# Gate blocks of a hybrid layer in a second lane beside the differential heads

## The chip, the cores and the metric

The kernel runs on one core of a Trainium2 chip. The metric is the device time of one execution in microseconds. TensorE's matmuls stand as PE in the profile and its weight loads as PEld; VectorE is DVE, ScalarE is ACT, GpSimd is POOL, and SP issues the DMAs.

## The reference

A sequence of 1024 tokens with 1024 features goes through two hybrid layers and then through two layers of a second block (S5 and stick-breaking attention, an MLP, gates and a pooling mixer). The change is in the hybrid layers alone. Each of them does this:

```python
h = rms_norm(x, norm_g) * (1.0 + scale) + shift
proj = h @ w_in                                  # 1024 x 3360
c_q, c_kv, k_pe, na_qkv, diff_qkv, g_mla, g_na, g_diff = split(proj)
...                                              # 6 MLA heads, 6 neighborhood heads, 4 differential heads
a = softmax(q0 @ k0) - lam * softmax(q1 @ k1)    # each differential head has two score maps
...
y = concat([o_mla * silu(g_mla), o_na * silu(g_na), o_d * silu(g_diff)]) @ w_out
return x + gate * y
```

The three gates are the last 1024 columns of `proj`: eight blocks of 128 features. Blocks 0 to 2 belong to the MLA heads, 3 to 5 to the neighborhood heads, 6 and 7 to the differential heads.

## The kernel before

All products are computed in fp32 by splitting each operand into a rounded part and a rest (`fp32r`), and three matmuls stand for one (`mm3`). A weight block is loaded (`wr`), its rounded part is a cast on ACT (`wh`, line 293) and its rest a subtraction on POOL (`wl`, line 294). The normalized input `hT` is held in 16 of the 43 pages of 4 KB per partition that the pool `pg` has; PSUM holds two score buffers of two banks (`big`, tile S) and four single banks (`mm`, also used for transposes and products).

A layer is a list of stages, and a stage is a list of items, generators whose parts are separated by `yield`. `lane` starts one item per turn and moves the items begun earlier on by one part, so that work of several items interleaves. While a stage's items run, the preparation steps of the next stage (loads and splits of its weights) are emitted, spread over those items. `run` can emit a second lane beside the first (`side`): its steps are spread evenly over the items of a given number of stages of the first lane. Up to now only a later part of the network uses it. From this emission the framework makes the order in which each engine is served, using times that it estimates (`schedule_with_timeline_sim=True`); the order is then fixed, each engine works through its own list, and the framework puts in the waits.

The stages of a hybrid layer in order: latent projections (`lat`); two gate stages of four blocks each, in which an MLA projection item (`mla_item`) alternates with two gate items (`gate_item`, lines 682 to 695); values and queries and keys of the other heads (`dv`, `dqk`, `nq`, `nk`, `nv`); the four differential heads, the six neighborhood heads, the six MLA heads; the output projection. A gate item takes 24 matmuls of 128x512 for one block and one half of the tokens, copies the product on ACT (line 691), computes the sigmoid (lines 340 to 345: two DVE operations and three activations), multiplies (line 693) and stores the gate to DRAM, from where the heads load it per pair of heads. Gate weights come as two halves of 512 columns, each in four loads of 512 KB.

A differential head has 16 items, one for each block of 128 queries and each of its two score maps: two matmuls of 512 columns into a score buffer (line 1070), the minimum on DVE, which also frees the buffer (line 790), the exponential on ACT (line 793), scaling on POOL (line 798) or DVE (line 1080), the addition of the two maps on POOL (line 1077), then, `lag` turns later, eight transposes (line 813) with copies on ACT (line 819), and, `lag2` turns after those of the second query block, the product with the values (line 839).

Of the kernel before, what the change touches and what calls it, by code (L numbers as in the profile page):

```python
# [9 lines left out]
F32 = mybir.dt.float32  # L10
F32R = mybir.dt.float32r
# [7 lines left out]
NT = 8  # L19
EPS = 1e-6  # L20

LEAD = {0: 4, 1: 8}
TABLES = "natural_log_exp_and_others"

CM = 3
# [79 lines left out]
class Weights:  # L105
# [12 lines left out]
    def load(self, j):  # L118
        N = self.N
        raw = self.new(F32, (128, self.kper, self.cols), name="wr")  # L120
        self.raw[j] = raw
        self.parts(raw, j * self.kper, self.kper)
# [38 lines left out]
class Net:  # L161
# [518 lines left out]
            self.dma(dst[t], v)  # L680
        return f

    def gate_item(self, W, b, n, hT, dst):
        def f():
            bs = slice(b * 128, b * 128 + 128)
            p = self.mm()
            self.mm3(p, [(W.hi(k)[:, bs], W.lo(k)[:, bs], hT.half("h", k, n), hT.half("l", k, n)) for k in range(8)])
            yield
            x = self.half(name="gx")
            g = self.half(name="gate")  # L690
            self.nc.scalar.copy(x, p)
            yield from self.sigmoid(g, x)
            self.nc.vector.tensor_mul(g, x, g)
            self.dma(dst[:, n * 512:n * 512 + 512], g)
        return f

    def project1(self, i, hT, early=None):
        I = self.I
        w_in = I["w_in"][i]
        D = {k: self.scratch(s, F32, name=f"{k}{i}") for k, s in {  # L700
            "mq": [6, 2, 96, S], "mk": [6, 2, 96, S], "mv": [NT, 128, 768],
            "nq": [2, 3, 128, S], "nk": [2, 3, 128, S], "nv": [NT, 128, 768],
            "dqk": [2, 4, 128, S], "dv": [NT, 128, 256], "g": [8, 128, S]}.items()}
        L = {}
# [19 lines left out]
        prep = []  # L724
# [9 lines left out]
        W = W0 = self.weights(w_in[:, 0:416], 416)  # L734
# [5 lines left out]
        else:  # L740
            ws.insert(0, gains)
        stages = [Stage(ws, [self.lat_item(t, hT, W, L) for t in range(NT)], "lat")]
        for c in (1, 0):
            W = self.weights(w_in[:, 2336 + c * 512:2848 + c * 512], 512)
            items = []
            for b in range(4):
                items += [self.mla_item((1 - c) * 4 + b, L, D)]
                items += [self.gate_item(W, b, n, hT, D["g"][c * 4 + b]) for n in range(2)]
            stages.append(Stage((prep if c else []) + W.steps(1), items, f"gate{c}", LEAD[c]))
        W = self.weights(w_in[:, 2080:2336], 256)  # L750
        stages.append(Stage(W.steps(), [self.v_plain(t, hT, W, 4, D["dv"]) for t in range(NT)], "dv"))

# [13 lines left out]
        stages.append(Stage(W.steps(), qk(W, 384, heads((0, 6, 64, "nk", False)), D["nk"]), "nk"))  # L766
        W = self.weights(w_in[:, 1184:1568], 384)
        stages.append(Stage(W.steps(), [self.v_item(t, hT, W, 6, D["nv"]) for t in range(NT)], "nv"))
        return D, stages


    def head_rows(self, src, h, d, ws, name):
# [264 lines left out]
    def diff_stages(self, i, D, mixT):  # L1037
# [45 lines left out]
        def sub(M):  # L1083
# [8 lines left out]
            yield  # L1092
            nc.vector.tensor_mul(M, M, sq)
            nc.vector.tensor_scalar_mul(M, M, C["sg"])
        st = self.attn_stages(4, 6, loads, tile, self.full_pair, D["dv"], D, mixT, sub=sub, subs=2, plain=True, lag=9, lag2=3)
        st[0].prep.insert(0, consts)
        return st

# [58 lines left out]
    def block1(self):  # L1157
# [17 lines left out]
            C["A"], C["B"] = self.rows(I["ln_mix_even_2"][0], "mA"), None  # L1175
        P, loads, products, ends = self.ada_rows()
        early = []
        D, st = self.project1(0, hT, early)

        begun = {}  # L1180

# [9 lines left out]
        stages = [Stage(pre, [lambda t=t: begun.pop(t) if t in begun else norm0(t) for t in range(NT)], "norm")]  # L1191
        for i in range(2):
            if i == 1:
                D, st = self.project1(i, hT)
            nf, E = self.na_bias(i)
            st[3].prep += nf
            stages += st
            if i == 0:
                ad = self.ada_steps(0, mods[0], (2,)) + self.ada_steps(1, mods[1])
                for j in range(4, 8):  # L1200
                    st[j].prep += ad[(j - 4) * len(ad) // 4:(j - 3) * len(ad) // 4]
            mixT = FeatT(self, "mx")
            df = self.diff_stages(i, D, mixT)
            na = self.na_stages(D, mixT, E)
            ml = self.mla_stages(D, mixT)
            if i == 1:
                T = self.s5_scratch()
                tb, steps = self.s5_tables(T)
                steps = [steps[j * 5:j * 5 + 5] for j in range(4)]
                for j in range(4):  # L1210
                    st[4 + j].prep = self.mixed(st[4 + j].prep, tb[j * len(tb) // 4:(j + 1) * len(tb) // 4])
                df[0].prep += steps[0]
            stages += df + na + ml
            hs = self.scratch([S, 1024], name=f"h{i}")
            setattr(self, f"h{i}", hs)
            nhT = FeatT(self, "hT")

            def fin(t, h, nhT=nhT, hs=hs):
                self.dma(hs[t * 128:t * 128 + 128], h)
                yield  # L1220
                x = yield from self.norm_scale(h, C["A"], C["B"])
                yield
                self.turn(x, t, nhT)

            so = self.out_stages(I["w_out"][i], mixT, lambda: C["gate"], src, fin)
            if i == 1:
                so[1].prep += steps[1]
                self.s5_later = [("v1", steps[2]), ("q0", steps[3])]
            so[0].prep.insert(0, lambda i=i: ldgate(i))
            so[1].prep.append((lambda: ldm(1)) if i == 0 else ldln)  # L1230
            stages += so
            src, hT = hs, nhT
# [786 lines left out]
```

## Time and the profile before

| | us |
|---|---|
| median of 3 runs | 4148.19 |
| lowest and highest | 4141.77, 4148.37 |
| the profiled execution | 4151.35 |
| its span | 4149.5 |
| PE busy in the span | 3929.7 |
| DVE busy | 2608.3 |
| ACT busy | 1831.4 |
| POOL busy | 1830.1 |

Busy times are sums over the whole span, and stages differ much, so what a stage is worth is read from windows over that stage. Records of matmuls overlap one another, so that PE's busy time contains more than the time that the array needs; the distance between starts tells that.

### The profile page before, as it was taken

The numbers are of one execution on the slowest core, as the hardware profiler recorded it, in microseconds if no ns is written. First come the engines' busy times: TensorE is split into PE (matmuls) and PEld (weight loads), VectorE is DVE, ScalarE is ACT, GpSimd is POOL, SyncE is SP. The second block draws the span as 40 slices with busy tenths as digits, with TensorE's granted clock in tenths as the row PEclk, the third lists the DMA queues.
The fourth block names the chain that finished last, engine by engine and source line by source line (L and its number), as shares of the span: only waits on it lengthen the run. The fifth ranks groups of instructions, "written<-read, shape, count | busy, mean of one in ns | idle before, by whom it ended". The sixth has DMA issues, their size and how long they took to land. (4 is left out here: it accounts for less than half of the span.)

```text
span 4149.5 us, 59427 instructions
## 1 busy us (share of the span) xinstructions
PE 3929.7 (95%) x21519; PEld 3353.5 (81%) x21519; DVE 2608.3 (63%) x5041; ACT 1831.4 (44%) x3867; POOL 1830.1 (44%) x1514
## 2 busy tenths in 40 slices
PE   7999889999998899999978999999999899999999
PEld 6889568989887579888867878888879888888879
DVE  6768768836886778655578644545575744455573
ACT  5643677726434877432365432111125621111145
POOL 2542765544433854612257444344433154444432
PEclk9999999999999999998799999999999999999999
DMA  5457434234635243335244311111111111111111
GB/s 180 139 194 234 121 92 131 88 124 122 181 105 166 74 140 92 117 121 186 87 157 137 123 51 51 47 46 56 46 49 55 42 47 51 51 44 53 56 42 56
DMA packets 379517, 410.47 MB, mean 99 GB/s; under 512 B 68265, under 2 KB 304457, under 8 KB 379224
## 3 DMA queue, kind: packets, MB, share of 16 engines
q1 hardware_dynamic: 379224, 406.67, 31.7%
q8 instruction: 171, 2.80, 0.3%
q14 instruction: 122, 1.00, 0.1%
HBM read 300.43 MB, written 106.18 MB: 98 GB/s over the span
## 5 line engine op out<-in xcount | busy, mean ns | idle before, releaser
L294 POOL TENSOR_TENSOR wl<-wr,wh 128x1024 fp32r<-128x1024 f32 (+4 forms) x262 | 606.6, 2321 | 1148.7 <-ACT wh L293 730.6
L1801 DVE TENSOR_TENSOR h<-h,mm 128x512 f32<-128x512 f32 x512 | 351.8, 687 | 657.1 <-PE mm L289 657.0
L289 PE MATMUL S<-hT,wh 128*128 128x512 f32 x2176 | 689.0, 390 | 3.8 <-ACT hT L297 1.5
L289 PE MATMUL S<-wh,hT 128*128 128x256 f32 (+3 forms) x2304 | 564.9, 330 | 6.8 <-DVE vst L298 3.1
L293 ACT CAST wh<-wr 128x1024 fp32r<-128x1024 f32 (+4 forms) x264 | 262.3, 1000 | 499.7 <-PE tp L289 247.0
L289 PEld LDWEIGHTS S<-hT,wh 128*128 128x128 f32 x2176 | 408.6, 188 | 90.7 <-ACT hT L297 2.3
L289 PEld LDWEIGHTS S<-wh,hT 128*128 128x128 f32 x2304 | 407.2, 195 | 21.2 <-issue 6.9
L289 PE MATMUL S<-hT,wl 128*128 128x512 f32 x1088 | 424.2, 390 | 0.0
L289 PE MATMUL S<-wl,hT 128*128 128x256 f32 (+3 forms) x1152 | 375.2, 326 | 0.6 <-POOL wl L294 0.6
L1801 DVE TENSOR_TENSOR h<-h,tp 128x512 f32<-128x512 f32 x512 | 351.8, 687 | 21.7 <-PE tp L289 21.7
L1785 ACT ACTIVATE z<-S 128x512 f32<-128x512 f32 x128 | 69.6, 595 | 632.0 <-PE S L289 631.9
L813 PE MATMUL tp<-c,P 128*128 128x128 f32 x2000 | 290.8, 280 | 37.7 <-DVE PTl L298 17.9
L798 POOL TENSOR_SCALAR P<-P,sx 128x1024 f32<-128x1024 f32 (+2 forms) x232 | 230.0, 997 | 215.7 <-DVE sx L794 87.6
L298 DVE TENSOR_TENSOR PTl<-tp,PTh 128x512 fp32r<-128x512 f32 (+3 forms) x432 | 253.2, 608 | 88.4 <-ACT PTh L297 84.9
L813 PEld LDWEIGHTS tp<-c,P 128*128 128x128 f32 x2000 | 234.6, 143 | 87.5 <-issue 21.7
L790 DVE CUSTOM_DVE_ANT_1 P<-S,zero 128x1024 f32<-128x1024 f32 x224 | 266.5, 1216 | 29.4 <-PE S L1070 28.3
L793 ACT ACTIVATE P<-P,sx 128x1024 f32<-128x1024 f32 x224 | 258.6, 1158 | 39.9 <-DVE sx L790 28.9
L297 ACT CAST PTh<-tp 128x512 fp32r<-128x512 f32 (+3 forms) x432 | 215.6, 529 | 117.2 <-PE tp L813 114.2
L289 PEld LDWEIGHTS S<-hT,wl 128*128 128x128 f32 x1088 | 204.6, 188 | 42.3
L289 PEld LDWEIGHTS S<-wl,hT 128*128 128x128 f32 x1152 | 224.6, 195 | 6.2 <-POOL wl L294 0.9
L289 PE MATMUL mm<-wh,hT 128*128 128x256 f32 x1152 | 221.5, 285 | 2.2 <-DVE hT L298 1.7
L835 PE MATMUL mm<-PTh,V 128*128 128x256 f32 (+1 forms) x784 | 209.2, 295 | 8.9 <-ACT PTh L297 6.4
(451 smaller groups left out, 9420.3 us busy)
## 6 DMA issues: line engine op xcount, KB each, us to landing
wr<-in_w_mlp_up_dram SPq DMA_DIRECT2D x64, 512.0 KB
wr<-in_w_mlp_down_dram SPq DMA_DIRECT2D x64, 512.0 KB
adw<-in_ada_w_dram SPq DMA_DIRECT2D x48, 512.0 KB
h<-h SPq DMA_DIRECT2D x32, 512.0 KB
wr<-in_w_in_dram SPq DMA_DIRECT2D x28, 512.0 KB
wr<-in_w_in_dram SPq DMA_DIRECT2D x24, 384.0 KB
mqT<-mq SPq DMA_DIRECT2D x24, 384.0 KB
mkT<-mk SPq DMA_DIRECT2D x24, 384.0 KB
```

Of the source, the lines that this page charges most:

```text
L289: self.nc.tensor.matmul(ps, a, b, start=(i == 0), stop=(i == n - 1))
L293: self.nc.scalar.copy(hi, src)
L294: (eng or self.nc.gpsimd).tensor_sub(lo, src, hi.bitcast(F32))
L297: self.nc.scalar.copy(hi, ps)
L298: self.nc.vector.tensor_sub(lo, ps, hi.bitcast(F32))
L790: nc.vector.tensor_tensor_reduce(P.rearrange("p (a b) -> p a b", a=2), Sv, self.zero.unsqueeze(2).to_broadcast([128, 2, 512]), 1.0, 3.0e38 ...
L793: nc.scalar.activation(P, P, AF.Exp, bias=nm[:, 0:1], scale=-1.0, accum_out=nm[:, 1:2])
L798: self.nc.gpsimd.tensor_scalar(P, P, f, g, op0=ALU.mult, op1=ALU.mult)
L813: self.nc.tensor.transpose(tp[:, j, :], P[:, b * 128:b * 128 + 128], self.eye)
L835: self.nc.tensor.matmul(*m, start=(j == 0), stop=(j == len(mms) - 1))
L1785: nc.scalar.activation(z, p[:, n, :], AF.Relu)
L1801: nc.vector.tensor_add(H[t][:, sl], H[t][:, sl], o)
```

## The change

Gate weights come in eight blocks of 128 columns with one load each, instead of two halves. Three blocks (6, 7, 3) stay in stages of their own in front of `dv`, where MLA items and gate items alternate. The other five (4, 5, 0, 1, 2) go into a second lane that starts with the first differential head, behind two empty turns, and is spread over the 64 items of the four heads. The lags of the differential heads become 5 and 2 instead of 9 and 3. In the first layer the steps that compute the next modulation rows are mixed evenly between the weight steps of the same stages instead of standing behind them. `hT` stays in its pages until the last gate item has read it.

```diff
--- before.py
+++ after.py
@@ -19,7 +19,7 @@
 NT = 8
 EPS = 1e-6
 
-LEAD = {0: 4, 1: 8}
+GATES = (6, 7, 3), (4, 5, 0, 1, 2)
 TABLES = "natural_log_exp_and_others"
 
 CM = 3
@@ -680,20 +680,6 @@
             self.dma(dst[t], v)
         return f
 
-    def gate_item(self, W, b, n, hT, dst):
-        def f():
-            bs = slice(b * 128, b * 128 + 128)
-            p = self.mm()
-            self.mm3(p, [(W.hi(k)[:, bs], W.lo(k)[:, bs], hT.half("h", k, n), hT.half("l", k, n)) for k in range(8)])
-            yield
-            x = self.half(name="gx")
-            g = self.half(name="gate")
-            self.nc.scalar.copy(x, p)
-            yield from self.sigmoid(g, x)
-            self.nc.vector.tensor_mul(g, x, g)
-            self.dma(dst[:, n * 512:n * 512 + 512], g)
-        return f
-
     def project1(self, i, hT, early=None):
         I = self.I
         w_in = I["w_in"][i]
@@ -740,13 +726,6 @@
         else:
             ws.insert(0, gains)
         stages = [Stage(ws, [self.lat_item(t, hT, W, L) for t in range(NT)], "lat")]
-        for c in (1, 0):
-            W = self.weights(w_in[:, 2336 + c * 512:2848 + c * 512], 512)
-            items = []
-            for b in range(4):
-                items += [self.mla_item((1 - c) * 4 + b, L, D)]
-                items += [self.gate_item(W, b, n, hT, D["g"][c * 4 + b]) for n in range(2)]
-            stages.append(Stage((prep if c else []) + W.steps(1), items, f"gate{c}", LEAD[c]))
         W = self.weights(w_in[:, 2080:2336], 256)
         stages.append(Stage(W.steps(), [self.v_plain(t, hT, W, 4, D["dv"]) for t in range(NT)], "dv"))
 
@@ -766,7 +745,53 @@
         stages.append(Stage(W.steps(), qk(W, 384, heads((0, 6, 64, "nk", False)), D["nk"]), "nk"))
         W = self.weights(w_in[:, 1184:1568], 384)
         stages.append(Stage(W.steps(), [self.v_item(t, hT, W, 6, D["nv"]) for t in range(NT)], "nv"))
-        return D, stages
+        g = [self.gate_stages(w_in[:, 2336:3360], bs, hT, D["g"]) for bs in GATES]
+        k = 0
+        for j, st in enumerate(g[0]):
+            st.items = [x for it in st.items for x in (None, it)] + [None]
+            if j == len(g[0]) - 1:
+                st.items.pop()
+            for e in range(0, len(st.items), 2):
+                st.items[e] = self.mla_item(k, L, D)
+                k += 1
+        assert k == NT
+        g[0][0].prep[:0] = prep
+        return D, stages[:1] + g[0] + stages[1:], g[1]
+
+    def gate_stages(self, w, bs, hT, dst):
+
+        R, W = {}, {}
+
+        def load(b):
+            R[b] = self.page(F32, (128, 8, 128), name="wr")
+            self.dma(R[b], w[:, b * 128:b * 128 + 128].rearrange("(k p) f -> p k f", p=128))
+
+        def split(b):
+            W[b] = [self.page(F32R, (128, 8, 128), name="w" + x) for x in "hl"]
+            self.split_sb(*W[b], R.pop(b))
+
+        def item(b, n):
+            def f():
+                p = self.mm()
+                h, l = W[b]
+                self.mm3(p, [(h[:, k, :], l[:, k, :], hT.half("h", k, n), hT.half("l", k, n)) for k in range(8)])
+                if n == 1:
+                    del W[b]
+                yield
+                x = self.half(name="gx")
+                g = self.half(name="gate")
+                self.nc.scalar.copy(x, p)
+                yield from self.sigmoid(g, x)
+                self.nc.vector.tensor_mul(g, x, g)
+                self.dma(dst[b][:, n * 512:n * 512 + 512], g)
+            return f
+        out = []
+        for j, b in enumerate(bs):
+            pre = ([lambda b=b: load(b)] if j == 0 else []) + [lambda b=b: split(b)]
+            if j + 1 < len(bs):
+                pre.append(lambda b=bs[j + 1]: load(b))
+            out.append(Stage(pre, [item(b, n) for n in range(2)], f"gate{b}"))
+        return out
 
 
     def head_rows(self, src, h, d, ws, name):
@@ -1092,7 +1117,7 @@
             yield
             nc.vector.tensor_mul(M, M, sq)
             nc.vector.tensor_scalar_mul(M, M, C["sg"])
-        st = self.attn_stages(4, 6, loads, tile, self.full_pair, D["dv"], D, mixT, sub=sub, subs=2, plain=True, lag=9, lag2=3)
+        st = self.attn_stages(4, 6, loads, tile, self.full_pair, D["dv"], D, mixT, sub=sub, subs=2, plain=True, lag=5, lag2=2)
         st[0].prep.insert(0, consts)
         return st
 
@@ -1175,7 +1200,7 @@
             C["A"], C["B"] = self.rows(I["ln_mix_even_2"][0], "mA"), None
         P, loads, products, ends = self.ada_rows()
         early = []
-        D, st = self.project1(0, hT, early)
+        D, st, gates = self.project1(0, hT, early)
 
         begun = {}
 
@@ -1191,14 +1216,14 @@
         stages = [Stage(pre, [lambda t=t: begun.pop(t) if t in begun else norm0(t) for t in range(NT)], "norm")]
         for i in range(2):
             if i == 1:
-                D, st = self.project1(i, hT)
+                D, st, gates = self.project1(i, hT)
             nf, E = self.na_bias(i)
-            st[3].prep += nf
+            st[4].prep += nf
             stages += st
             if i == 0:
                 ad = self.ada_steps(0, mods[0], (2,)) + self.ada_steps(1, mods[1])
-                for j in range(4, 8):
-                    st[j].prep += ad[(j - 4) * len(ad) // 4:(j - 3) * len(ad) // 4]
+                for j in range(4):
+                    st[5 + j].prep = self.mixed(st[5 + j].prep, ad[j * len(ad) // 4:(j + 1) * len(ad) // 4])
             mixT = FeatT(self, "mx")
             df = self.diff_stages(i, D, mixT)
             na = self.na_stages(D, mixT, E)
@@ -1208,8 +1233,9 @@
                 tb, steps = self.s5_tables(T)
                 steps = [steps[j * 5:j * 5 + 5] for j in range(4)]
                 for j in range(4):
-                    st[4 + j].prep = self.mixed(st[4 + j].prep, tb[j * len(tb) // 4:(j + 1) * len(tb) // 4])
+                    st[5 + j].prep = self.mixed(st[5 + j].prep, tb[j * len(tb) // 4:(j + 1) * len(tb) // 4])
                 df[0].prep += steps[0]
+            df[0].side = ([Stage([], [None] * 2)] + gates, len(df))
             stages += df + na + ml
             hs = self.scratch([S, 1024], name=f"h{i}")
             setattr(self, f"h{i}", hs)
```

## Rows read from the trace of the kernel before

**Rows 1.** The head of the page.

```profile
span 4149.5 us, 59427 instructions
```

**Rows 2.** Windows: length, busy us (instructions) of each engine, TensorE clock, DMA.

```profile
107.00:232.00 125.00, 119.69 (x614) 102.53 (x613) 88.88 (x171) 75.47 (x171) 56.46 (x81) 0.97 0.49 145
423.00:565.00 142.00, 120.58 (x563) 74.47 (x562) 105.54 (x211) 110.04 (x200) 108.53 (x71) 0.95 0.35 92
450.00:500.00 50.00, 46.33 (x229) 28.99 (x228) 39.04 (x80) 41.63 (x76) 41.88 (x27) 1.00 0.26 59
1298.00:1434.00 136.00, 115.15 (x542) 71.14 (x539) 105.09 (x210) 106.64 (x194) 104.55 (x69) 0.96 0.39 99
565.00:679.00 114.00, 101.38 (x675) 86.60 (x674) 82.69 (x222) 84.07 (x194) 65.18 (x78) 0.94 0.44 131
679.00:831.00 152.00, 151.53 (x1037) 137.43 (x1037) 127.86 (x254) 116.55 (x215) 81.50 (x68) 1.00 0.30 92
```

**Rows 3.** Timeline of PE in a gate item: start, us, instruction.

```profile
161.04 0.62 PE L289 MATMUL mm<-hT,wh 128*128 128x512 f32 x2
...
164.44 0.62 PE L289 MATMUL mm<-hT,wh 128*128 128x512 f32 x2
```

**Rows 4.** Timeline in the differential heads: start, us, instruction.

```profile
499.76 1.27 DVE L1080 SCALAR_TENSOR_TENSOR P<-P,sx 128x1024 f32<-128x1024 f32 x1
...
504.07 1.04 PE L813 MATMUL tp<-c,P 128*128 128x128 f32 x8
...
505.04 3.67 PE L839 MATMUL mm<-PTp,V 128*64 128x256 f32 x16
...
507.97 2.37 POOL L1077 TENSOR_TENSOR P<-P 128x1024 f32<-128x1024 f32 x1
508.04 3.38 DVE L1080 SCALAR_TENSOR_TENSOR P<-P,sx 128x1024 f32<-128x1024 f32 x1 [3.66 <-POOL P L798]
```

**Rows 5.** Groups of the differential heads' window, busy us, mean ns, idle before.

```profile
L790 DVE CUSTOM_DVE_ANT_1 P<-S,zero 128x1024 f32<-128x1024 f32 x63 | 75.4, 1216 | 13.8 <-PE S L1070 13.0 <-POOL P L1077 0.2
...
L839 PE MATMUL mm<-PTp,V 128*64 128x256 f32 x208 | 51.3, 394 | 0.0
L1070 PE MATMUL S<-dkT,dqT 128*128 128x512 f32 x128 | 45.9, 457 | 16.1 <-DVE sx L790 16.0
...
L813 PE MATMUL tp<-c,P 128*128 128x128 f32 x220 | 32.7, 284 | 4.4 <-ACT PTp L819 1.9 <-POOL P L1077 1.8 <-ACT M L919 0.6
L819 ACT COPY PTp<-tp 128x512 f32<-128x512 f32 x55 | 29.6, 588 | 5.8 <-PE tp L813 5.8
...
L1080 DVE SCALAR_TENSOR_TENSOR P<-P,sx 128x1024 f32<-128x1024 f32 x11 | 19.3, 1756 | 3.7 <-POOL P L798 3.7
```

**Rows 6.** Waits in the differential heads: total us, times, longest.

```profile
PE S L1070 <- DVE sx L790: 16.0, 17, 3.1
DVE P L790 <- PE S L1070: 13.0, 13, 2.6
```

**Rows 7.** Groups of the gate and MLA items' window.

```profile
L294 POOL TENSOR_TENSOR wl<-wr,wh 128x1024 fp32r<-128x1024 f32 x7 | 17.3, 2483 | 14.1 <-ACT wh L293 10.3 <-issue 3.8
L344 DVE SCALAR_TENSOR_TENSOR gate<-gx,gate 128x512 f32<-128x512 f32 x14 | 13.2, 945 | 8.0 <-ACT gate L342 8.0
L693 DVE TENSOR_TENSOR gate<-gx,gate 128x512 f32<-128x512 f32 x14 | 12.2, 873 | 3.2 <-ACT gate L345 3.2
...
L341 ACT ACTIVATE gate<-gate 128x512 f32<-128x512 f32 x14 | 8.9, 634 | 13.5 <-DVE gate L340 12.7 <-DMA mq<-mTl 0.6
...
L691 ACT COPY gx<-mm 128x512 f32<-128x512 f32 x15 | 8.7, 578 | 5.4 <-PE mm L289 5.4
...
L340 DVE TENSOR_SCALAR gate<-gx 128x512 f32<-128x512 f32 x15 | 7.4, 496 | 3.8 <-ACT gx L691 3.7
...
L293 ACT CAST wh<-wr 128x1024 fp32r<-128x1024 f32 x6 | 6.3, 1044 | 1.3 <-DMA wr<-in_w_in_dram 1.3
```

**Rows 8.** The gate tile, all its instructions: duration min/median/max in ns.

```profile
L344 DVE SCALAR_TENSOR_TENSOR gate<-gx,gate x32: 673/692/2470, 117.8 to 1108.2; 128x512 f32<-128x512 f32 x32
```

## Prediction

> **What bounds the kernel now.** I read the profile from the outside in. The head of the page gives the span, 4149.5 us [rows 1]; the profiled execution took 4151.35 us, so 1.85 us lie around the span. The sum below is made against 4151.35; the median of the runs shown, 4148.19, is 3.2 us less. Then the stages: the first sight of a tile name in the trace bounds each, and the windows view gives the engines' busy time in it [rows 2]. The change touches two stages of each hybrid layer. Gate and MLA-projection items (107 to 232 us in layer 0): PE 119.69 of 125 us, DVE 88.88; PE sets the pace. Differential heads (423 to 565): no engine is full by its own instructions, ACT 110.04, POOL 108.53, DVE 105.54 of 142.
>
> PE's 120.58 there must be read with care, because the records of matmuls overlap. Starts tell more. Fifteen matmuls of 512 columns start within 164.44 - 161.04 = 3.40 us, 227 ns each [rows 3]. Eight transposes take 1.04 us, so (1.04 - 0.284)/7 = 108 ns; sixteen records of the plain PV product take 3.67, so (3.67 - 0.394)/15 = 218 ns [rows 4, 5]. The differential window holds 128 score matmuls, 220 transposes and 208 PV records [rows 5]: 128 x 0.227 + 220 x 0.108 + 208 x 0.218 = 29.1 + 23.8 + 45.3 = 98 us of true PE work in 142. So 44 us per layer are PE idle. The waits say why: PE waits for DVE to release a score buffer (16.0 us), DVE for PE's scores (13.0) [rows 6]; two score buffers pass back and forth among engines that serve in order. That idle is what gate matmuls could fill. How the static order packs them is what cannot be read here.
>
> **The change part by part.**
>
> *Removed from the gate stage.* Ten gate items per layer, each 24 matmuls: 10 x 24 x 0.227 = 54.5 us of PE. They take their DVE work along, 0.496 + 0.945 + 0.873 = 2.31 us each [rows 7], 23.1 us. What stays: PE 119.7 - 54.5 = 65.2, DVE 88.9 - 23.1 = 65.8. The two are level, and eight MLA items now have six gate items between them instead of sixteen, so their DVE chains have less cover. The most that DVE shows beside a full PE is the MLA heads, 127.86 of 152, 84% [rows 2]. 65.8/0.84 = 78 us: the stage gives back 47. Bounds: 54.5 if PE stays the bound (70.5 us), and 32 if DVE stays at today's 71% (93 us). I take 47, since the mix is nearest to the MLA heads.
>
> *Added to the differential heads.* PE 54.5 us. ACT per item one copy 0.578 and three activations of 0.63, 2.47, ten of them 24.7; and five casts of a weight block of 128x1024 at 1.044, 5.2. POOL five subtractions at 2.48, 12.4 [rows 7]. DVE ten times 0.496 and two operations of one shape, of which the first has a median of 0.69 [rows 7, 8].
>
> Those two read two SBUF tiles each, and beside a busy POOL that costs. The add-and-scale of the heads, also with two SBUF inputs, takes 1.27 us alone and 3.38 when it starts 0.07 us after a POOL add of 2.37, whose end it waits out; its mean is 1.756, 0.49 over the undisturbed one [rows 4, 5]. Priced by that row, a gate item is 0.50 + 2 x (0.69 + 0.49) = 2.86, ten of them 28.6 us.
>
> The Trainium skill, SBUF — State Buffer, section "SBUF: two separate sides", says that DVE and GpSimd share one port pair as an exclusive lock: a DVE operation with two SBUF inputs and a GpSimd operation that reads SBUF shut each other out for a whole instruction. The 3.38 us row agrees. By that rule, at its worst, every such operation would wait out a whole POOL instruction, and the move into the stage where POOL is busiest would be wrong; that is the fourth case below, from rows.
>
> *The shorter lags.* 9 + 3 becomes 5 + 2: transposes and PV come five items sooner, so five items' worth moves from the neighborhood stage into this one: PE 5 x (4 x 0.108 + 4 x 0.218) = 6.5, ACT 5 x 0.588 = 2.9. The neighborhood stage (101.38 of 114 PE, ACT 84.07) is full on no engine, so I give it back 3 us, between 0 and 6.5. P tiles live four items less, which makes room among the 43 pages for the 16 pages of hT that now live on through the heads and for three to five pages of gate weights.
>
> *The new load of the heads.* PE 98 + 54.5 + 6.5 = 159, ACT 110.0 + 24.7 + 5.2 + 2.9 = 142.8, DVE 105.5 + 28.6 = 134, POOL 108.5 + 12.4 = 121. PE becomes the longest, ACT is close. Now ACT's share is 77% over the window and 83% in its best stretch (41.63 of 50) [rows 2]; with 80% the stage takes 142.8/0.80 = 178.5, PE then at 89%. It grows by 36. Bounds: +18 if PE runs without a hole, as in the MLA heads (151.53 of 152), and +61 if every gate burst of 24 matmuls simply adds to the stage (54.5 + 6.5). I take 36.
>
> *What I cost at nothing.* Weight blocks of 128 columns come in 512-byte rows; the bytes are the same, DMA is busy 35% in the heads [rows 2], and each load but the first is emitted a block ahead of its split. If that cover failed, a split would hold ACT and POOL for a landing. The adaptive rows mixed between weight steps change the order of the same work in the four stages between; PE and DVE do the same there in another order, and I give it 0, plus or minus 3. On SP's queue five weight loads and ten gate stores pass behind head loads that are a head ahead.
>
> *Sum.* Per layer -47 + 36 - 3 = -14. The second layer's heads (136 us, DVE 105.09, ACT 106.64 [rows 2]) hold the same work, so twice: -28. 4151.35 - 28 = 4123.3, against the median 4120.
>
> **The rivals.**
>
> *PE fills nearly every hole.* For it: the MLA heads keep PE at 151.53 of 152 us with DVE at 84%. Then the heads grow by 18 to 24, the gate stage gives 50 to 54, the layer gains about 34: 4148 - 68 = 4080. Against it: ACT would have to reach 142.8/163 = 88%, and no row has it above 83.
>
> *No change: the gain is given back.* ACT stays at today's 77%: 142.8/0.775 = 184, +42. DVE in the shorter gate stage reaches 77% only: 65.8/0.77 = 85.5, 39.5 back. -39.5 + 42 - 3 is nothing: 4148. For it: neither share is better today. Against: today's window includes the heads' start, and the shorter lag mends part of that.
>
> *Slower: bursts instead of filling.* Twenty-four matmuls stand in PE's queue in one piece, 5.45 us. Two score buffers feed DVE for 2 x 1.216 us; then DVE, ACT and POOL run dry, and the next scores come late. If a burst costs over 4.4 us of its 5.45, the heads grow by more than 50 (43.5 and the lag's 6.5) and the layer loses. At the full price, with the gate stage at -40: -40 + 61 - 3 = +18 a layer, 4184. For it: the waits between PE and DVE over the score buffers, 29 us already. Against it: 44 us of PE idle that the bursts can overlap.
>
> *Slower: DVE behind POOL.* If the twenty two-input operations wait out a POOL add each, a gate item costs DVE 0.50 + 2 x (0.69 + 2.37) = 6.6, ten 66; DVE 171.5/0.84 = 204, the heads grow by 62, the layer by 12: 4172. It decides from a mean wait of about 1.9 us, (192 x 0.84 - 105.5 - 5 - 13.8)/20; the rows show 0.49.
>
> **How the numbers follow.** Forecast 0.40 (its own range 4098 to 4140), more filled 0.14, given back 0.17, bursts 0.19, DVE behind POOL 0.10. The time is the forecast's, 4120. The range 4078 to 4182 leaves out the better half of the filled case and the far ends of the slower ones, about 2 in 10. A measurement of this kernel can tell about 0.2%, 8 us, from no change: three runs spread 6.6 us. Faster: forecast and filled, 0.54, with a little of the given-back case 0.55; same: most of that case, 0.15; slower 0.30.
>
> **What would show it.** Right: the matmuls of six gate items between the latent projections and `dv`, that stage near 78 us, DVE near 84% in it; the heads near 178 us with PE by pitch near 89%, ACT near 80%; means of the gate's two-input operations near 1.2 us in the heads; the neighborhood stage 3 us shorter. Wrong, and each names its step: a gate stage over 85 us (DVE), heads over 192 (bursts: PE waits for DVE's score buffer in long single waits right after a gate item), two-input means over 2.5 us (POOL), or a hole in front of the first neighborhood scores, because its loads found no free page while hT was still held; I gave that no price.

## The result and the profile after

| | before | after |
|---|---|---|
| median, us (runs) | 4148.28 (4) | 4168.90 (4) |
| lowest and highest | 4141.77, 4153.25 | 4166.74, 4173.44 |
| profiled execution | 4151.35 | 4173.44 |

The ratio is 1.0051, with a 95% interval of 1.0039 to 1.0063: the change makes the kernel 0.5% slower, 20.6 us. I had predicted 28 us faster, so 49 us have to be found.

I bounded the stages in both traces by the same instructions and give their lengths in us for each layer:

| | before 1 | after 1 | before 2 | after 2 | predicted per layer |
|---|---|---|---|---|---|
| gate stage: first to last gate matmul ahead of `dv` | 124.7 | 77.8 | 125.9 | 75.1 | -47 |
| stretch: from there to the first score matmul of the heads | 191.3 | 214.1 | 193.2 | 202.7 | 0 |
| differential heads: first to last score matmul | 141.5 | 186.5 | 135.9 | 186.7 | +36 |
| neighborhood, with the gap in front | 113.7 | 110.5 | 113.5 | 109.2 | -3 |
| MLA heads | 153.3 | 153.2 | 154.2 | 154.1 | 0 |

The first gate matmul comes 4.4 us earlier in the first layer (102.9 instead of 107.3). All this sums to about +18 us. The code behind the two layers is unchanged; there the profiles of all my runs differ by up to 12 us, so the times below are medians, where they are not said to be of one run, and the stages are read one by one.

Here is the windows view of the kernel after (length, then busy us and instructions of PE, PE's weight loads, DVE, ACT, POOL; the granted clock; DMA share; GB/s). The rows are gate stage, stretch, heads and neighborhood of the first layer, then gate stage, stretch and heads of the second; [rows 2] holds their counterparts before, except for the second gate stage.

```profile
103.00:181.00 78.00, 67.90 (x354) 58.87 (x353) 64.81 (x132) 46.98 (x122) 38.96 (x71) 0.91 0.51 147
181.00:395.00 214.00, 196.33 (x1088) 174.50 (x1087) 149.50 (x272) 71.06 (x179) 68.50 (x52) 0.95 0.66 213
395.00:581.00 186.00, 173.40 (x810) 122.02 (x809) 130.42 (x237) 136.31 (x243) 119.21 (x75) 0.95 0.32 84
581.00:692.00 111.00, 98.63 (x664) 84.97 (x663) 85.13 (x226) 84.98 (x196) 70.09 (x80) 0.94 0.55 158
992.00:1067.00 75.00, 66.91 (x353) 58.01 (x352) 61.10 (x128) 47.29 (x122) 35.80 (x66) 0.91 0.52 148
1067.00:1270.00 203.00, 191.55 (x1122) 178.07 (x1121) 161.27 (x531) 70.49 (x177) 64.81 (x57) 0.97 0.54 161
1270.00:1457.00 187.00, 173.54 (x815) 123.30 (x814) 131.31 (x238) 136.46 (x245) 122.21 (x75) 0.96 0.33 89
```

The stretch between was not among my rows. The same view of the kernel before, of the two stretches and, between them, the second gate stage:

```profile
232.00:423.00 191.00, 187.16 (x1069) 170.55 (x1068) 140.34 (x263) 70.90 (x174) 64.18 (x48) 0.99 0.71 229
979.00:1105.00 126.00, 120.45 (x610) 102.73 (x609) 93.07 (x178) 76.46 (x172) 59.02 (x83) 0.97 0.50 145
1105.00:1298.00 193.00, 186.04 (x1101) 175.21 (x1101) 151.62 (x509) 68.08 (x170) 56.63 (x44) 0.98 0.53 158
```

Four things are to be seen. In the gate stage DVE reaches 64.81/78 = 83%, as predicted. In the stretch the number of matmuls is nearly the same, but PE is idle for 17.7 of 214 us, where it was idle for 3.8 of 191; the other 9 us of its growth are PE's busy time, at a granted clock of 0.95 instead of 0.99. In the heads ACT is at 136.31/186 = 73%, where I had put 80%. And PE, which was without an instruction for 142 - 120.58 = 21.4 us of the heads [rows 2], is so for 186 - 173.40 = 12.6 us.

Groups of the heads' window after, to be read against [rows 5]:

```profile
L815 DVE CUSTOM_DVE_ANT_1 P<-S,zero 128x1024 f32<-128x1024 f32 x63 | 75.8, 1217 | 28.5 <-PE S L1095 28.3 <-issue 0.2
...
L864 PE MATMUL mm<-PTp,V 128*64 128x256 f32 x216 | 51.8, 391 | 0.2 <-ACT PTp L844 0.2
L289 PE MATMUL mm<-hT,wh 128*128 128x512 f32 x160 | 50.5, 394 | 0.5 <-ACT M L944 0.5
L1095 PE MATMUL S<-dkT,dqT 128*128 128x512 f32 x126 | 45.4, 453 | 7.3 <-DVE sx L815 7.2
...
L838 PE MATMUL tp<-c,P 128*128 128x128 f32 x224 | 32.6, 286 | 2.8 <-POOL P L1102 2.8
L289 PE MATMUL mm<-hT,wl 128*128 128x512 f32 x80 | 31.2, 390 | 0.0
...
L1105 DVE SCALAR_TENSOR_TENSOR P<-P,sx 128x1024 f32<-128x1024 f32 x11 | 17.9, 1627 | 3.7 <-POOL P L823 3.7
...
L344 DVE SCALAR_TENSOR_TENSOR gate<-gx,gate 128x512 f32<-128x512 f32 x10 | 12.3, 1230 | 1.7 <-ACT gate L342 1.7
...
L785 DVE TENSOR_TENSOR gate<-gx,gate 128x512 f32<-128x512 f32 x9 | 8.4, 937 | 1.2 <-ACT gate L345 1.2
```

The minimum on DVE (now L815) takes as long as before, but DVE waits 28.3 us for PE's scores instead of 13.0, and PE waits 7.2 us for DVE instead of 16.0 [rows 6]. PE's idle was filled in part, and DVE paid for it. In the same window the ten times of the first of the gate's two-input operations, shortest, median and longest in ns:

```profile
L344 DVE SCALAR_TENSOR_TENSOR gate<-gx,gate x10: 673/814/2623, 444.6 to 574.0; 128x512 f32<-128x512 f32 x10
```

### The profile page after: what moved, and what is told of

It reads as the page before. It is cut to its first block, busy times and chain, and to the rows that moved or that the text cites. A ratio compares the mean times of both kernels' runs of the same rounds, so it can differ in the third digit from the quotient of the medians.

```text
span 4171.6 us, 59409 instructions
## 1 busy us (share of the span) xinstructions
PE 3946.7 (95%) x21519; PEld 3370.7 (81%) x21519; DVE 2623.4 (63%) x5041; ACT 1828.2 (44%) x3867; POOL 1825.2 (44%) x1514
## 4 chain that ended last, share of the span: by engine, by line
PE 74%; DVE 11%; ACT 5%; issue 4%; POOL 3%; DMA 3%; SPq 1%; POOLq 0%; DVEq 0%; ACTq 0%
PE S L289 31%; PE mm L289 17%; PE tp L289 8%; PE tp L838 3%; PE mm L860 3%; PE S L976 3%; PE mm L864 2%; DMA adw<-in_ada_w_dram 1%; PE tp L368 1%; PE S L1095 1%; POOL P L823 1%; PE S L1621 1%; PE S L1036 1%; POOL wl L294 1%; DVE xn L357 1%
## 5 line engine op out<-in xcount | busy, mean ns | idle before, releaser
L289 PE MATMUL S<-wl,hT 128*128 128x256 f32 (+3 forms) x1152 | 377.4, 328 | 12.7 <-POOL wl L294 12.6
L815 DVE CUSTOM_DVE_ANT_1 P<-S,zero 128x1024 f32<-128x1024 f32 x224 | 267.4, 1217 | 55.7 <-PE S L1095 54.7
```

The lines of the kernel that those rows point to most:

```text
L289: self.nc.tensor.matmul(ps, a, b, start=(i == 0), stop=(i == n - 1))
L815: nc.vector.tensor_tensor_reduce(P.rearrange("p (a b) -> p a b", a=2), Sv, self.zero.unsqueeze(2).to_broadcast([128, 2, 512]), 1.0, 3.0e38 ...
```

## The experiments

Two losses are to be explained. For the stretch, theory M says that the mixed adaptive rows cost it, and its rival C that the shorter gate stage no longer covers the loads and splits behind it. For the heads the candidates are bursts of 24 matmuls, the elementwise work, PSUM banks, pages and the lag; later on, E says that every gate matmul costs the heads the same, and K that the cost is not spread evenly. The letters of the other theories belong to the expectation in which they stand; the M in the run with both parts left out is not the M of the mixing.

Each kernel is the one after, or the one before, with the edit shown or named; `...` stands for lines of an edit that are not shown. Times are medians; a ratio is that to the kernel before on the same chip.

**The mixed adaptive rows.** First the change without its mixing:

```diff
-                    st[5 + j].prep = self.mixed(st[5 + j].prep, ad[...])
+                    st[5 + j].prep += ad[...]
```

> The changed kernel, with the adaptive-row steps of layer 0 behind the weight steps again, as before the change. Theory M (the mixing puts 512 KB row loads between the weight loads of the next stage, so weights land late): the stretch from the last gate matmul in front of dv to the first score matmul in layer 0 falls from 214 us to about 195, the time by 12 to 20 us to about 4152. Rival C (the gate stage is 47 us shorter and no longer covers the loads of dv and dqk, whatever their order): the stretch stays above 208 and the time within 5 us of 4169.

4148.54 us, ratio 1.0005 (0.9995 to 1.0015). So inside the change the mixing costs about 20 us, all of the loss. Of that, 12.4 us are seen in the first layer's stretch (214.1 to 201.7, where M had 195). Then the mixing alone, put into the kernel before:

> The kernel before, with nothing changed but the adaptive-row steps of layer 0 mixed between the weight steps. Theory M: its stretch from the last gate matmul to the first score matmul grows from 191 us by 10 to 20, and the time to about 4160. Rival C: the stretch and the time stay within 4 us of before, as the long gate stage still covers the loads.

4150.42 us, 1.0010 (0.9999 to 1.0021). The stretch grows by 9.1 us there too, but the time as a whole moves by some 0.1%. In its profile the neighborhood stage behind is 4.5 us shorter and the second layer's stretch 3.6, so that the growth doesn't reach the end; why is open. So M holds for the place but not for the time of about 4160, and the full 20 us belong to the mixing together with the rest of the change.

The place is the same in both. This is POOL's timeline after (start, us, instruction, idle before), where the weights of `nq` are split:

```profile
285.44 1.89 POOL L657 TENSOR_TENSOR hx<-hx,dqg 128x256 f32<-128x256 f32 x1 [17.41 <-DVE hss L334]
...
290.90 2.03 POOL L294 TENSOR_TENSOR wl<-wr,wh 128x768 fp32r<-128x768 f32 x1
295.03 2.39 POOL L657 TENSOR_TENSOR hx<-hx,nqg 128x384 f32<-128x384 f32 x2 [2.10 <-DVE hx L535]
303.33 1.01 POOL L657 TENSOR_TENSOR hx<-hx,nqg 128x384 f32<-128x384 f32 x1 [5.91 <-DVE hr L335]
...
307.52 4.56 POOL L294 TENSOR_TENSOR wl<-wr,wh 128x768 fp32r<-128x768 f32 x2
...
313.61 2.78 POOL L294 TENSOR_TENSOR wl<-wr,wh 128x768 fp32r<-128x768 f32 x1
```

and in the kernel without the mixing:

```profile
272.92 2.06 POOL L294 TENSOR_TENSOR wl<-wr,wh 128x768 fp32r<-128x768 f32 x1 [6.64 <-DMA wr<-in_w_in_dram]
276.99 3.66 POOL L294 TENSOR_TENSOR wl<-wr,wh 128x768 fp32r<-128x768 f32 x2 [2.01 <-ACT wh L293]
...
284.11 1.84 POOL L294 TENSOR_TENSOR wl<-wr,wh 128x768 fp32r<-128x768 f32 x1
```

The four splits are through at 286 us without the mixing and at 316 with it. With the mixing they stand later on POOL's list: the first behind normalizations of `dqk` rows, which wait 17.41 us for DVE, the second and third behind normalizations of `nq` rows, which wait for DVE again, and the fourth behind one more. The four weight loads are issued at 272.03, 275.51, 280.66 and 294.93 with adaptive loads between them, against 268.74 to 273.11 without one; but after the change no wait of POOL at these splits is put down to a load, so what shows is the position on POOL. On PE's timeline after, three matmuls wait for these splits:

```profile
309.39 0.44 PE L289 MATMUL S<-wl,hT 128*128 128x384 f32 x1 [1.22 <-POOL wl L294]
...
310.02 0.34 PE L289 MATMUL S<-wl,hT 128*128 128x384 f32 x1
...
312.14 0.44 PE L289 MATMUL S<-wl,hT 128*128 128x384 f32 x1 [1.44 <-POOL wl L294]
...
316.44 0.69 PE L289 MATMUL S<-wl,hT 128*128 128x384 f32 x1 [2.41 <-POOL wl L294]
...
317.57 0.53 PE L289 MATMUL S<-wl,hT 128*128 128x384 f32 x1
```

With the mixing alone they wait at the same place, in the same way:

```profile
345.89 0.44 PE L289 MATMUL S<-wl,hT 128*128 128x384 f32 x1 [1.21 <-POOL wl L294]
...
348.64 0.44 PE L289 MATMUL S<-wl,hT 128*128 128x384 f32 x1 [1.44 <-POOL wl L294]
...
352.96 0.69 PE L289 MATMUL S<-wl,hT 128*128 128x384 f32 x1 [2.98 <-POOL wl L294]
```

Windows around it, after and then without the mixing:

```profile
300.00:320.00 20.00, 14.93 (x78) 13.67 (x77) 15.95 (x30) 8.04 (x20) 11.30 (x7) 0.83 0.50 143
```

```profile
300.00:320.00 20.00, 20.00 (x114) 18.07 (x113) 16.50 (x32) 5.92 (x17) 4.91 (x4) 1.00 0.73 220
```

In the same 20 us PE starts 78 instructions instead of 114. The named waits are only 5 us; the granted clock is 0.83 in these 20 us, and behind the last wait a matmul of 384 columns takes 0.53 us, where one ahead of it took 0.34.

**The five blocks on the first lane.** They follow as stages of their own behind the three, and there is no second lane:

```diff
-        return D, stages[:1] + g[0] + stages[1:], g[1]
+        return D, stages[:1] + g[0] + g[1] + stages[1:], []
...
-            df[0].side = ([Stage([], [None] * 2)] + gates, len(df))
```

> The changed kernel, with the five gate blocks as stages of the first lane behind the other three instead of in the second lane; lags and mixing as changed. Theory S (the second lane's gate items cost the heads nearly all that they cost in front): the heads fall from 187 us to about 142 or less, the gate stage grows from 78 to about 132, and the time changes by less than 10 us. Rival (the heads' growth is the shorter lags or the pages that hT holds, not the gate items): the heads stay above 160.

4192.47 us, 1.0106 (1.0091 to 1.0121). The heads take 153.0 and 152.2, the gate stage 138.7 and 139.3. Theory S, with 142 us or less and a time within 10 us, falls, and so does its rival with over 160. The growth of the heads from 153 to 186 comes with the second lane, that is, with the gate items, their loads and splits and the pages that they hold; the lane is worth 23 us against this placement, in which five gate stages have no MLA items beside them.

**The lags alone**, in the kernel before:

```diff
-        ... plain=True, lag=9, lag2=3)
+        ... plain=True, lag=5, lag2=2)
```

> The kernel before, with the lags of the differential heads at 5 and 2 alone. As the prediction had it: the heads 6 us longer, the neighborhood stage 3 shorter, the time within 5 us of 4148. Rival (short lags make PE wait for POOL and DVE in order): the heads over 150 us in each layer and the time above 4160.

4153.11 us, 1.0012 (1.0002 to 1.0022). Heads +8.4 and +12.9, neighborhood -8.3 and -8.1 with its gap: work moves, and a little is lost; the heads and the neighborhood together are as long as before in the first layer and 4.8 us longer in the second. The other way, lags 9 and 3 in the change without the mixing:

> The kernel of a_nomix with the lags of the differential heads back at 9 and 3. Theory L (the short lags make PE, which serves in order, wait for POOL's and DVE's part of the softmax; alone they made the heads 8 and 13 us longer): the heads fall from 185 us by 8 or more, the neighborhood stage grows by 5 to 9, the time falls by 2 to 8. Rival P (hT, the gate weights and the longer-lived P tiles together need more than 43 pages): the heads do not get shorter, or the first neighborhood scores come over 5 us after the last scores of the heads.

4156.11 us, 1.0010 (1.0000 to 1.0020); the heads stay at 186.3 and 187.9. Beside the gate items the lag is worth nothing.

**What of a gate item costs the heads?** Halves of 12 matmuls with a turn between them, without the mixing:

```diff
...
+                    self.mm3(p, t[:4], True, False)
+                    yield
+                    self.mm3(p, t[4:], False, True)
...
```

> The kernel of a_nomix with each gate item of the second lane emitted in two halves of 12 matmuls, one per turn, and twice as many turns. Theory B (a piece of 24 matmuls, 5.45 us, outlasts the two score buffers, which feed DVE for 2.4 us; the rest of the piece stops the heads): with 2.7 us a piece the heads fall from 185 us by 10 to 20 in each layer and the time by 20 to 35, to about 4120. Rival A (the heads are held by the sum of ACT's and DVE's work, or by the PE work itself): the heads stay within 5 us of 185.

4152.26 us, 1.0017 (1.0006 to 1.0028); heads 188.1 and 196.9, against 184.5 and 186.4 without the halving. Half the length gains nothing.

Without the sigmoid and the multiplication in the second lane:

> The changed kernel, with the gate's sigmoid and multiplication left out in the second lane: each of its gate items only copies its product on ACT and stores that. It leaves out ten times 1.9 us of ACT and 2.6 us of DVE per layer. Theory B: the heads fall by less than 8 us from 187, since the matmul pieces stay. Rival A (ACT's and DVE's added work, with the waits behind POOL): they fall by 15 to 25.

One run, 4155.76 us; heads 184.3 and 186.1, shorter by 2.2 and 0.6. The neighborhood stages behind them are 5 and 3 us shorter too.

With 3 of the 24 matmuls of each of its items (`for k in range(1)`):

> The changed kernel, with 21 of the 24 matmuls of each gate item in the second lane left out (one of eight blocks of the contraction is kept); loads, splits, activations and multiplications stay. It leaves out 47.7 us of PE per layer. Theory B: the heads fall from 187 us to within 5 us of the 149 of the kernel with short lags alone. Rival A: they stay above 165.

One run, 4116.26 us; heads 169.7 and 162.2, shorter by 16.8 and 24.5 for 10 x 21 x 0.227 = 47.7 us of PE work taken out. Theory B had the heads near 149 and its rival above 165, and neither holds in both layers.

PSUM banks were the next suspect: the copy follows the matmuls in the same turn, so that a bank comes free sooner (without the mixing):

```diff
...
-                yield
+                if b not in GATES[1]:
+                    yield
...
```

> The kernel of a_nomix with the copy of a second-lane gate product emitted right behind its matmuls instead of one turn (13 us) later. Theory T (the product holds one of four single PSUM banks for a turn, and transposes and value products wait for the other three): the heads fall from 185 us by over 8 in each layer. Rival (banks are free in time): they change by less than 4.

4153.00 us, 1.0014 (1.0003 to 1.0025); heads 190.8 and 194.8, so an earlier copy gains nothing. In the trace after, no wait of PE's matmuls in the heads is put down to the copy of a gate product either.

Pages: in the kernel before, a small item late in the heads keeps `hT` alive, with 16 matmuls that read all its pages.

```diff
...
+            df[0].side = ([Stage([], [None] * 12 + [hold])], len(df))
```

> The kernel before, with 16 matmuls added late in the differential heads that read every page of hT into one PSUM bank, so that its 16 pages stay taken, and one copy of that bank; nothing else. The added work is 3.6 us of PE. Rival P (pages): the heads grow from 142 and 136 us by over 10, or a hole of over 5 us stands in front of the neighborhood scores. Otherwise pages are no part of the cause: they grow by less than 6.

One run, 4151.61 us; heads 143.0 and 143.5, +1.5 and +7.6, of which its own matmuls are 3.6. The pages of `hT` explain little of 45 and 51; those of the gate weights were not tested apart.

Then the missing corner, the 21 matmuls and the sigmoid both left out, and the middle, half of the matmuls with everything else kept (`range(4)`):

> The changed kernel with both left out in the second lane: 21 of 24 matmuls, and the sigmoid with its multiplication. Loads, splits, three matmuls, one copy and the store stay, and hT stays in its pages. Theory M (either load alone fills the slack of the heads, PE's with matmuls, ACT's, DVE's and POOL's without): the heads come to 150 to 156 us, near the 149 of the kernel with short lags alone, so that the sigmoid costs 10 to 15 us beside few matmuls and next to nothing beside many. Rival W (the loads, splits and the pages of hT cost it): they stay at 160 or more.

> The changed kernel with 12 of the 24 matmuls of each gate item of the second lane left out (four of eight blocks of the contraction are kept), the sigmoid as it is; 27.2 us of PE less per layer. Theory K (PE is full from some point on): the first nine matmuls added to the three of e_nomm, 20.4 us, lengthen the heads by less than 5 to about 170, and the last twelve then by 15 or more. Rival E (every matmul pushes the scores back by the same part): about 176, half way between 166 and 187.

One run each, 4104.59 and 4132.72 us; heads 160.0 and 158.7, and 174.2 and 177.6. Means of the two layers, the lower rows from the first score of the heads to the last of the neighborhood:

| us | 3 matmuls | 12 | 24 |
|---|---|---|---|
| heads, without sigmoid | 159.4 | | 185.2 |
| heads, with it | 166.0 | 175.9 | 186.6 |
| heads and neighborhood, without | 265.5 | | 290.8 |
| heads and neighborhood, with it | 273.3 | 284.1 | 296.5 |

The lag alone gives 149.4 for the heads. Loads, splits, held pages, copies and three matmuls add 10, near W's 160 and not M's 150 to 156 of that expectation. The sigmoid adds 6.6 to the heads beside few matmuls and 1.4 beside all; with the neighborhood it is 7.8 and 5.7, so most of that difference is work that moves between the two stages. The 21 other matmuls add 20.7: 9.9 for the first nine (20.4 us of PE work), 10.7 for the next twelve (27.2). That is 0.4 to 0.5 of their own time, and about 0.5 with the neighborhood counted.

The mean fits E. The layers one by one do not: the first nine matmuls add 4.5 us to the heads of the first layer and 15.3 to those of the second, the next twelve 12.4 and 9.2, so the first layer is near K and the second its opposite. With one run of each kernel it is not shown that the cost is even; what is shown is that the 21 matmuls cost a third to a half of their own time (16.8 and 24.5 of 47.7). The waits of the first layer's heads with 3 matmuls show the exchange:

```profile
PE S L1095 <- DVE sx L815: 17.2, 15, 2.4
DVE P L815 <- PE S L1095: 13.7, 11, 3.0
```

and with all 24:

```profile
DVE P L815 <- PE S L1095: 28.3, 21, 4.2
...
PE S L1095 <- DVE sx L815: 7.2, 9, 2.2
```

PE's waits for a score buffer fall by 10 us, DVE's waits for scores rise by 14.6, and the first layer's heads grow by 16.8. That a gate matmul outside PE's waits holds back a score for which DVE is ready is a reading, and it isn't shown: in the trace after, gate matmuls run in or just ahead of only about 12 of the 28 us.

**Earlier weights.** In the stretch something remains above before, 10.4 and 8.2 us, without the mixing too. It lies at its start: there PE is busy for 42.45 of 49 us after and for 40.80 of 48 without the mixing, and was for 48.31 of 49 before.

```profile
181.00:230.00 49.00, 42.45 (x272) 36.36 (x271) 32.51 (x36) 14.93 (x30) 20.09 (x18) 0.90 0.90 321
```

```profile
182.00:230.00 48.00, 40.80 (x276) 35.36 (x274) 21.61 (x33) 17.24 (x35) 20.46 (x19) 0.93 0.79 268
```

```profile
232.00:281.00 49.00, 48.31 (x304) 42.02 (x303) 31.41 (x36) 19.21 (x37) 23.20 (x16) 1.00 0.89 311
```

By C, the shorter gate stage covers less of the weight loads of `dv` and `dqk`. The run with the five blocks on the first lane bears it out: behind its gate stage of 139 us the second layer's stretch is 192.7 us, as before, and the first's, still mixed, 205.0 instead of 214.1. So I had both weights prepared a stage earlier (without the mixing):

```diff
+        dv, dqk = stages[1:3]
+        g[0][-1].prep += dv.prep
+        dv.prep, dqk.prep = dqk.prep, []
```

> The kernel of a_nomix with the weight steps of dv and dqk each emitted one stage earlier (dv's beside gate block 7, dqk's beside gate block 3). Theory C (behind a gate stage of 78 us instead of 125 the loads of dv and dqk start too late): the time from the first dv copy to the first dqk copy falls from 40 and 42 us to about 28 and 33, the time by 15 to 22 to about 4130. Rival (dv itself is held by DMA, which is busy 0.9 there, whenever its loads are emitted): that time stays above 38 in layer 0.

4153.93 us, 1.0018 (1.0005 to 1.0032). From the first copy of `dv` to that of `dqk` it is 32.1 and 30.6 us instead of 40.3 and 41.6, but `dv` itself starts 4.0 and 6.5 us later behind the last gate matmul, and the second gate stage is 5.5 longer. The wait moved, and the 4130 that C expected did not come.

**An earlier start of the second lane.** Its first block is loaded and split among the steps ahead of the heads, and the two empty turns fall away (without the mixing):

```diff
-            df[0].side = ([Stage([], [None] * 2)] + gates, len(df))
+            df[0].prep += gates[0].prep
+            gates[0].prep = []
+            df[0].side = (gates, len(df))
```

> The kernel of a_nomix with the first gate block of the second lane loaded and split one stage earlier and without the two empty turns, so that gate matmuls start with the fifth or sixth item of the heads instead of the thirteenth. Theory H (the holes that gate matmuls can fill are those at the heads' start, where PE waits for the first softmax; later the PE queue is nearly full): the heads fall from 185 us by 6 to 12 in each layer, the time by 10 to 20, to about 4133. Rival B (holes are spread evenly): the heads change by less than 4.

4142.26 us, 0.9984 (0.9974 to 0.9993): faster than the kernel before, though the heads are no shorter (188.1 and 186.2) and the theory that expected that falls. The first gate item's copy comes 5.7 us behind the first score, where after it comes 43.5 behind. Where the time is gained stays open: at the end of the second layer its profile is 3 us ahead of the one without the mixing, the net of gains and losses of up to 8 us in single stages.

On top of that, three blocks in the second lane instead of five; eight gate items of the first lane have an MLA item in front:

```diff
-GATES = (6, 7, 3), (4, 5, 0, 1, 2)
+GATES = (6, 7, 3, 4, 5), (0, 1, 2)
...
```

> The kernel of n_start with three blocks (0, 1, 2) in the second lane and five in front, beside which the eight MLA items stand in front of the first eight gate items. If each moved item costs 3.7 us in the heads: they take about 171 us, and the gate stage about 100. The time then stays near the 4142 of n_start if the gate stage is bound by PE already, and falls to about 4130 if the last items moved cost more in the heads than the first (theory K).

4139.00 us, 0.9988 (0.9977 to 0.9998); heads 177.8 and 178.4, where 171 was expected, gate stage 92.3 and 93.2, where 100 was. It has the lowest median of the kernels that do all the work, but the kernel before is faster on its chip too (4147.59 against 4149.93), the two ratios' intervals overlap, and I don't call it better than the one above. Its stretches are 192.3 and 192.9 us, as before the change: a gate stage of 92 us covers what one of 75 to 78 doesn't, as C has it.

## Why the prediction was wrong

- **The gate stage: right.** Predicted 78 us by DVE at 84%; measured 77.8 and 75.1 at 83% and 81%.
- **The largest failed step: what I cost at nothing, the stretch between.** "The adaptive rows mixed between weight steps change the order of the same work in the four stages between ... and I give it 0, plus or minus 3." The stretch grew by 22.8 and 9.5 us, 32 of the 49. I counted work and not positions: the mixing puts adaptive loads between the weight loads on SP, and splits behind waiting normalizations on POOL, and PE waits for the splits. Taking it out brings back 12.4 us in its place and 20 us in all; in the profiles the other 7 lie in small parts, none over about 2 us, in the stages behind, and why they do is open. The rest of the 32, some 20 us, comes with the shorter gate stage, which uncovers loads of the next stages: with gate stages of 92 us or more the second layer's stretch is back at 193. I had not listed what the long gate stage hid.
- **The heads: direction right, size and its ground wrong.** The step "with 80% the stage takes 142.8/0.80 = 178.5" sized them by ACT. ACT reached 73%, and PE by pitch 126 x 0.227 + 224 x 0.108 + 216 x 0.218 + 240 x 0.227 = 154 of 186 us, 83% and not 89%. That is +45 and +51 instead of +36, 24 of the 49 us. Nor did ACT's share set the length: without the sigmoid ACT has some 19 us less to do, which by that formula makes the heads 24 us shorter, and they were 2.2 and 0.6 shorter, while without 21 of 24 matmuls they were 16.8 and 24.5 shorter. The room on PE was counted too large as well: of the "44 us per layer" that "are PE idle" by pitch, PE was without an instruction for 21.4, and 12.6 of these are left.
- **The sum.** The 24 and the 32 are 7 more than the 49; other terms gave back about as much, mainly a second gate stage 4 us shorter than forecast and 4.4 us ahead of the first. Price by price, the lag was 8 to 13 and not 6.5, and the neighborhood gave back 8 of that in its own run.
- **The signs.** None of the four signs of being wrong came: the gate stage is under 85 us, the heads under 192, the two-input means under 2.5, and the first neighborhood scores follow the heads within 0.3 us. The largest loss lay where no sign was set.
- **The gain given back:** this rival had the heads nearly right (184), but not the gate stage, which gave its 47 and more.
- **The price of the lock: right.** L344 takes 1.23 us on the mean in the first layer, where I had 1.18 and the rival needed over 2.5. The Trainium skill, SBUF — State Buffer, "SBUF: two separate sides", says that a DVE operation with two SBUF inputs is blocked for the whole of a GpSimd instruction that reads SBUF and started first. The ten times in the first layer's heads, from 0.67 to 2.62 us, fit that, but only four of them are over 1.5 us. Without the sigmoid and multiplication the heads were 2.2 and 0.6 us shorter, and 7.6 and 3.9 with the neighborhood, far from the 62 of that rival; so DVE behind POOL is ruled out as the main cause.
- **Bursts:** this rival had the sign of the change in time, and heads near its 192 us, but half the piece gave no shorter heads, and its own sign, long single waits of PE for a score buffer, did not come: the longest is 2.2 us and was 3.1 [rows 6]. Its price of a full 54.5 is wrong too; the matmuls cost about half of their time.
- **Pages**, which had no price, needed next to none: little in the run that holds those of `hT`.
- **Still open:** why a static order with about 32 us of PE idle by pitch, 12.6 of it without an instruction, can't take the gate matmuls for less than 0.4 to 0.5 of their time. Shorter pieces, longer lags and an earlier copy gained nothing, and the pages of `hT` cost little. An order with gate matmuls only where PE waits for a buffer was not tried.

## What to carry to other kernels

Shortening a stage uncovers what it hid: before crediting the gain, list the loads and splits of the next two stages and where they stand in their queues. Steps that are mixed into another list cost nothing in work and much in position, so read each in-order queue that they pass. When an idle engine in a loop of several engines is to be filled, count the gaps in its busy row beside its idle time by pitch; here the filler cost about half of its time, and a smaller share moved did no worse: three blocks against five. Count the stage behind together with the one that is filled, since work moves between them.

## What the runs showed of the hardware

- TensorE's granted clock was lower where PE waited. In the gate stage it is 0.91 after and was 0.97; in the 20 us with three waits for splits it is 0.83, against 1.00 in the same 20 us without the mixing, where PE is busy throughout. Between its two levels (1.2 and 2.4 GHz), 0.83 is a third of the 20 us at the lower one. So waits of 5 us in all cost PE more than their own length there.
